# Batching the probability-times-value products of two attention layers over all query blocks of a pair of heads

## The chip, the cores and the metric

The kernel runs on one core of a Trainium2 chip. The metric is device time in microseconds (us) of one execution. Before the change, three runs took 2350.43, 2351.89 and 2341.58 us, median 2350.43. The execution that was profiled took 2338.97 us; its span from the first to the last instruction is 2337.0 us, so 1.97 us lie around the span.

## The reference, cut to what matters

A float32 network on 512 tokens of width 1024: a recurrent layer, an MLP, an attention layer with forget gates ("fox", 16 heads of 64), an MLP, a hybrid layer ("nsa", 8 query heads that share 2 key/value heads, in three branches, beside a short convolution), an MLP. The change touches the probability-times-value products of fox and of two of the three nsa branches. For one block of 128 queries fox computes

```python
logits = einsum('bhqd,bhkd->bhqk', q[:, :, s:e], k[:, :, :e]) * scale
logits = logits + (c[:, :, s:e, None] - c[:, :, None, :e])
p = softmax(where(causal, logits, -inf), axis=-1)
outs.append(einsum('bhqk,bhkd->bhqd', p, v[:, :, :e]))
```

so query block i sees the key blocks 0 to i. In nsa the selected branch picks all 8 blocks of 64 keys, and the window (512) covers the sequence; both are causal attention over the same 512 keys with different keys and values, a linear distance bias and a gate per query and head. The third branch attends to 31 compressed keys.

## The kernel before, in words

Activations lie feature-major, 128 features by 512 tokens in a tile. The large projections multiply fp32 data as three fp32r products (high by high, high by low, low by high): L146, L147, L149 in `proj_fm` with 512 moving columns, L266 to L268 in `proj_tm` with 256. Their weights arrive by DMA (`wr`) and are split into `wh` on ScalarE (L91, L95) and `wl` on VectorE (L92, L96).

Attention goes by pair of heads: 8 pairs in fox (`attend`), 4 in nsa (`nsa_attend`), where each pair runs the branches b = 0 (selected) and b = 1 (window). There are thus 8 + 8 = 16 groups, each of four query blocks i (128 queries) and two heads. One row of work, for one head and one query block of width (i+1) x 128 keys, is: two score products into PSUM bank "s" (L497/L498, L743/L744); VectorE adds the bias and takes the minimum (L331); ScalarE takes the exponential (L339); VectorE the reciprocal (L342); GpSimd scales (L343); then `p_rows` transposes the i+1 blocks by fp32 products with the identity (L363) into bank "t" and copies them to a tile `pt` of 512 columns (6 buffers, L365), by ScalarE for the first head of the pair and by VectorE for the second. In fox GpSimd also builds the bias tile D (L500, L502). D, E and the broadcast gates cb share the 6 buffers of tag "sc".

After both heads of a query block, `pv2` (L373) multiplies: for each key block, for each of the two heads, one fp32 product of the 64 columns of V (stationary) with 128 columns of `pt` (moving). The two heads write to partitions 0 to 63 and 64 to 127 of the PSUM bank O. The trace records each fp32 product twice (two passes), so a query block has 4(i+1) records and a group 40. In nsa the compressed branch first writes O with one product of 512 columns for each head (L737, the tile `pc`, from the tag "pt"). When O is complete, `o_parts` splits it into a high part (ScalarE, L379) and a low part (VectorE, L380), which the output projection reads. O has one buffer.

The rows are interleaved with other work by generators: in fox with the projections of the following heads and, for the last two pairs, with the output projection `out1`; the rest of it, `out2`, comes after the last pair. In nsa each of the 32 yields of attention alternates with one of `nsa_conv`. The fox loop goes through i = 3, 2, 1, 0 with the heads inside; the nsa loop through i = 0 to 3 with b inside, and the transposes that prepare the next pair (`stack`) stand after i = 1 of branch 1. `stack` also issues four DMAs on SP.

The program text is not the order on the engines: the tile framework orders the instructions itself when the program is built, on a simulated timeline (L1666, `schedule_with_timeline_sim=True`), and sets the semaphores. Once built, each engine's order is fixed.

Of the kernel before, what the change touches and what calls it, by code (L numbers as in the profile page):

```python
# [9 lines left out]
F32 = mybir.dt.float32  # L10
# [8 lines left out]
P = 128  # L19
D = 1024  # L20
T = 512
# [10 lines left out]
class Net:  # L32
# [322 lines left out]
                next(fill, None)  # L355
                done += 1

    def p_rows(self, pool, E, n, eng):

        tb = self.bank("t")  # L360
        w = n * P
        for j in range(n):
            self.nc.tensor.transpose(tb[:, j * P:(j + 1) * P], E[:, j * P:(j + 1) * P], self.ident)  # L363
        pt = pool.tile([P, T], F32, tag="pt", bufs=6, name=self.nm("pt"))
        eng(pt[:, :w], tb[:, :w])  # L365
        return pt

    def pv2(self, O, n, V, pts, i, first=True, last=True):


        for b in range(n):
            for j in range(2):
                self.nc.tensor.matmul(O[64 * j:64 * j + 64, i * P:(i + 1) * P], V(j, b), pts[j][:, b * P:(b + 1) * P],  # L373
                                      start=first and b == 0, stop=last and b == n - 1)

    def o_parts(self, O, oh, ol):

# [4 lines left out]
    def fox(self):  # L382
        nc, tc, a = self.nc, self.tc, self.a
        with tc.tile_pool(name="fox", bufs=2, reuse_waits="tile") as fp, \
# [4 lines left out]
            f, u, s2, q = [fp.tile([P, 4 * H], F32, name=f"f{n}") for n in "fusq"]  # L389
# [57 lines left out]
            tb = self.bank("t")  # L447
# [5 lines left out]
            c = self.sc("fc")[:H]  # L453
# [4 lines left out]
            tb = self.bank("t")  # L458
# [17 lines left out]
            def attend(m):  # L476

                cc, j = divmod(m, 2)
                v = st["v", cc]
                ks, qs = st["kq", m]  # L480
                oh = fp.tile([P, T], F32R, tag="oh", bufs=NK, name=self.nm("oh"))
                ol = fp.tile([P, T], F32R, tag="ol", bufs=NK, name=self.nm("ol"))
                O8.append((oh, ol))
                cbs = []
                for hh in range(2):
                    cb = self.sc("cb")
                    nc.sync.dma_start(cb, cd[2 * m + hh:2 * m + hh + 1, :].partition_broadcast(P))
                    cbs.append(cb)
                O = self.bank("o")
                for i in range(3, -1, -1):  # L490
                    wd = (i + 1) * P
                    pts = []
                    for hh in range(2):
                        h = 2 * m + hh
                        S = self.bank("s")
                        qa, qb = qs[hh]
                        nc.tensor.matmul(S[:, :wd], qa[:, i * P:wd], ks[hh][:, :wd], start=True, stop=False)  # L497
                        nc.tensor.matmul(S[:, :wd], qb[:, i * P:wd], ks[hh][:, :wd], start=False, stop=True)  # L498
                        Dt = self.sc("D")
                        nc.gpsimd.tensor_scalar(Dt[:, :wd], cbs[hh][:, :wd], 1.0, nct[:, i * H + h:i * H + h + 1],  # L500
                                                op0=ALU.mult, op1=ALU.add)
                        nc.gpsimd.affine_select(Dt[:, i * P:wd], Dt[:, i * P:wd], pattern=[[-1, P]],  # L502
                                                compare_op=ALU.is_ge, fill=BIG, base=0, channel_multiplier=1)
                        E = self.softmax_row(fp, S, Dt[:, :wd], wd, 1.0)
                        pts.append(self.p_rows(fp, E, i + 1, nc.vector.tensor_copy if hh else nc.scalar.copy))
                        if hh:
                            self.pv2(O, i + 1, lambda c, b: v[:, b, 128 * j + 64 * c:128 * j + 64 * c + 64], pts, i)
                            if i == 0:
                                self.o_parts(O, oh, ol)
                        yield  # L510


# [168 lines left out]
    def nsa_attend(self, fp, e, O4):  # L681

        nc = self.nc
        gt, v = e["gt"], e["v"]
        qs = []

        def stack(m):
            qs.extend(self.q_stack(fp, self.fm_bank(e["q"][m // 2], (m % 2) * P, 256), e["gq"]))
        def compressed(h):

            g = h // 4
            qa, qb = qs[h]
            Dch = fp.tile([P, P], F32, tag="Dch", bufs=2, name=self.nm("Dch"))
            nc.gpsimd.tensor_scalar(Dch, e["Dc"].rearrange("p t c -> p (t c)"), 2.0 ** -(h + 1), 0.0, op0=ALU.mult,
                                    op1=ALU.add)
            S = self.bank("s")
            for i in range(4):
                r = slice(i * P, (i + 1) * P)
                o = S[:, 32 * i:32 * i + 32]
                nc.tensor.matmul(o, qa[:, r], e["kc"][g], start=True, stop=False)  # L700
                nc.tensor.matmul(o, qb[:, r], e["kc"][g], start=False, stop=True)
            E = fp.tile([P, P], F32, tag="Ec", bufs=2, name=self.nm("Ec"))
            E3 = E.rearrange("p (t c) -> p t c", t=4)
            m4 = fp.tile([P, 3, 4], F32, tag="m4", bufs=2, name=self.nm("m4"))
            nc.vector.tensor_tensor(E, S[:, :P], Dch, op=ALU.add)
            nc.vector.tensor_reduce(m4[:, 0], E3, axis=AX.X, op=ALU.min)
            nc.vector.tensor_scalar(m4[:, 0], m4[:, 0], 1e20, None, op0=ALU.min)
            nc.vector.tensor_tensor(E3, E3, m4[:, 0, :, None].to_broadcast([P, 4, 32]), op=ALU.subtract)
            nc.scalar.activation(E, E, AF.Exp, scale=-1.0)
            nc.vector.tensor_reduce(m4[:, 1], E3, axis=AX.X, op=ALU.add)  # L710
            nc.vector.tensor_scalar(m4[:, 1], m4[:, 1], 1e-30, None, op0=ALU.max)
            nc.vector.reciprocal(m4[:, 2], m4[:, 1])
            nc.vector.tensor_tensor(m4[:, 2], m4[:, 2], gt[:, :, h], op=ALU.mult)
            nc.vector.tensor_tensor(E3, E3, m4[:, 2, :, None].to_broadcast([P, 4, 32]), op=ALU.mult)
            tb = self.bank("t")
            for i in range(4):
                nc.tensor.transpose(tb[:32, i * P:(i + 1) * P], E3[:, i], self.ident)
            pc = fp.tile([P, T], F32, tag="pt", bufs=6, name=self.nm("pc"))[:32]
            nc.scalar.copy(pc, tb[:32])
            return pc  # L720

        stack(0)
        for hp in range(4):
            g = hp // 2
            hv = slice(g * 64, g * 64 + 64)
            Dh = []
            for h in (2 * hp, 2 * hp + 1):
                Dh.append(fp.tile([P, T], F32, tag="Dh", bufs=3, name=self.nm("Dh")))
                nc.gpsimd.tensor_scalar(Dh[-1], e["D0"], 2.0 ** -(h + 1), 0.0, op0=ALU.mult, op1=ALU.add)
            O = self.bank("o")  # L730
            for i in range(4):
                wd = (i + 1) * P
                for b in range(2):
                    if i == b == 0:
                        pcs = [compressed(h) for h in (2 * hp, 2 * hp + 1)]
                        for j in range(2):
                            nc.tensor.matmul(O[64 * j:64 * j + 64], e["vc"][:, hv], pcs[j], start=True, stop=False)  # L737
                    pts = []
                    for j in range(2):
                        h = 2 * hp + j  # L740
                        qa, qb = qs[h]
                        S = self.bank("s")
                        nc.tensor.matmul(S[:, :wd], qa[:, i * P:wd], e["ks"][b][g][:, :wd], start=True, stop=False)  # L743
                        nc.tensor.matmul(S[:, :wd], qb[:, i * P:wd], e["ks"][b][g][:, :wd], start=False, stop=True)  # L744
                        E = self.softmax_row(fp, S, Dh[j][:, T - wd:], wd, 1.0,
                                             gate=gt[:, i, 8 * (b + 1) + h:8 * (b + 1) + h + 1])
                        pts.append(self.p_rows(fp, E, i + 1, nc.vector.tensor_copy if j else nc.scalar.copy))
                    self.pv2(O, i + 1, lambda j, n: v[:, n, 128 * b + 64 * g:128 * b + 64 * g + 64], pts, i, first=False,
                             last=b == 1 and i == 3)
                    if i == 1 and b and hp < 3:  # L750
                        stack(hp + 1)
                    if i == 3 and b:
                        self.o_parts(O, *O4[hp])
                    yield
# [916 lines left out]
```

## Time and profile before

| what | value |
| --- | --- |
| three runs, median | 2350.43 us (2341.58 to 2351.89) |
| profiled execution / its span | 2338.97 / 2337.0 us |
| PE busy (matmul) | 2239.0 us, 96% |
| VectorE, ScalarE, GpSimd busy | 1367.7, 945.0, 568.1 us |
| DMA traffic | 237.37 MB, 102 GB/s on average |
| the chain that ended last | PE 82%, DVE 5%, DMA 2% |

PE is TensorE's matmul, PEld its weight load, DVE VectorE, ACT ScalarE, POOL GpSimd, SP SyncE. Matmuls overlap in the array and their ends are modelled, so the time from one start to the next tells more than the duration of a record. A timeline row merges like records that follow each other: the first number is the start, the second the length until the last one's end, and "xN" the count of records. The fox attention lies at about 905 to 1131 us of the span and the nsa attention at 1570 to 1830 us.

### The profile page before, as it was taken

Reading aid. Unit: us, or ns where it says so; the run is one execution under the profiler, and the core shown is the slowest. Engines: PE = TensorE matmul, PEld = TensorE weight load, DVE = VectorE, ACT = ScalarE, POOL = GpSimd, SP = SyncE. Lnnn points to the kernel's source line nnn. Section 1 sums busy time; section 2 is a strip of 40 time slices with the busy share of each in tenths; the row PEclk is TensorE's granted clock in tenths of the full one; section 3 lists DMA queues with packets and bytes.
Section 4 is the critical chain, followed back from the end, with each engine's and each line's share of the span. In section 5 each row is a group of like instructions: output and inputs, shape, how many; then the busy total and the mean of one; then the engine's idle time right before and its main releaser. Section 6 shows DMA issues by size and latency. Waiting matters only on the chain.

```text
span 2337.0 us, 33070 instructions
## 1 busy us (share of the span) xinstructions
PE 2239.0 (96%) x12545; PEld 1856.5 (79%) x12545; DVE 1367.7 (59%) x2718; ACT 945.0 (40%) x1928; POOL 568.1 (24%) x655
## 2 busy tenths in 40 slices
PE   4988877999999999999999999999999999999999
PEld 4767666778888889987788888897777888888887
DVE  8997778664444467765744444755554445444444
ACT  5575455343322345654523324344334324332331
POOL 6554235221021012444220120303331102012010
PEclk9998888999999999999999999999999999999999
DMA  3158634213232233332323223232223433223322
GB/s 124 39 163 252 176 94 131 65 41 106 90 105 93 92 102 108 98 83 71 104 93 105 91 95 104 75 116 73 84 84 104 135 108 109 90 90 100 99 91 81
DMA packets 104015, 237.37 MB, mean 102 GB/s; under 512 B 9664, under 2 KB 42176, under 8 KB 103856
## 3 DMA queue, kind: packets, MB, share of 16 engines
q1 hardware_dynamic: 73712, 214.28, 28.8%
q10 hardware_dynamic: 30144, 20.98, 3.0%
q8 instruction: 99, 1.62, 0.3%
q14 instruction: 60, 0.49, 0.1%
HBM read 210.02 MB, written 18.91 MB: 98 GB/s over the span
## 4 chain that ended last, share of the span: by engine, by line
PE 82%; DVE 5%; DMA 2%; ACT 1%; issue 1%; POOL 0%; ACTq 0%; SPq 0%; DVEq 0%; POOLq 0%
PE psacc L146 20%; PE psacc L149 20%; PE psacc L147 20%; PE pso L373 2%; PE psacc L268 2%; PE psacc L266 2%; PE psacc L267 2%; PE pst L363 2%; DVE wl L92 1%; PE pso L1447 1%; PE pso L1449 1%; PE pso L1448 1%; DMA xh<-in_x_dram 0%; PE pss L497 0%; PE pss L744 0%
## 5 line engine op out<-in xcount | busy, mean ns | idle before, releaser
L91 ACT CAST wh<-wr 128x512 fp32r<-128x512 f32 (+1 forms) x593 | 324.2, 617 | 470.7 <-PE psacc L149 341.2
L92 DVE TENSOR_TENSOR wl<-wr,wh 128x512 fp32r<-128x512 f32 (+1 forms) x581 | 422.1, 778 | 38.7 <-ACT wh L91 35.8
L146 PE MATMUL psacc<-xg,wh 128*128 128x512 f32 x1104 | 432.6, 392 | 0.0
L147 PE MATMUL psacc<-xg,wl 128*128 128x512 f32 x1104 | 432.1, 391 | 0.0
L149 PE MATMUL psacc<-xgl,wh 128*128 128x512 f32 x1104 | 431.2, 392 | 0.4 <-DVE xgl L176 0.4
L146 PE MATMUL psacc<-hid,wh 128*128 128x512 f32 x768 | 299.7, 393 | 0.0
L149 PE MATMUL psacc<-hidl,wh 128*128 128x512 f32 x768 | 299.1, 392 | 0.0
L147 PE MATMUL psacc<-hid,wl 128*128 128x512 f32 x768 | 298.5, 391 | 0.0
L254 POOL TENSOR_TENSOR xall<-xall,yt 128x512 f32<-128x512 f32 x72 | 107.7, 1495 | 666.3 <-DVE yt L253 666.3
L149 PEld LDWEIGHTS psacc<-xgl,wh 128*128 128x128 f32 x1104 | 207.2, 188 | 44.7 <-DVE xgl L176 1.5
L147 PEld LDWEIGHTS psacc<-xg,wl 128*128 128x128 f32 x1104 | 207.4, 188 | 42.4 <-issue 0.9
L146 PEld LDWEIGHTS psacc<-xg,wh 128*128 128x128 f32 x1104 | 207.4, 188 | 42.2 <-issue 0.5
L253 DVE TENSOR_TENSOR yt<-psacc,rb 128x512 f32<-128x512 f32 x96 | 66.4, 692 | 273.3 <-PE psacc L149 273.3
L241 DVE TENSOR_TENSOR ht<-ht,psacc 128x512 f32<-128x512 f32 x96 | 66.1, 688 | 224.2 <-ACT ht L240 224.0
L240 ACT ACTIVATE ht<-psacc 128x512 f32<-128x512 f32 x96 | 57.6, 600 | 280.2 <-PE psacc L149 280.1
L149 PEld LDWEIGHTS psacc<-hidl,wh 128*128 128x128 f32 x768 | 144.2, 188 | 32.7
L147 PEld LDWEIGHTS psacc<-hid,wl 128*128 128x128 f32 x768 | 144.2, 188 | 32.0
L146 PEld LDWEIGHTS psacc<-hid,wh 128*128 128x128 f32 x768 | 144.2, 188 | 31.5
L266 PE MATMUL psacc<-wh,xg 128*128 128x256 f32 (+2 forms) x504 | 144.3, 287 | 1.7 <-ACT gt L647 1.5
L268 PE MATMUL psacc<-wh,xgl 128*128 128x256 f32 (+2 forms) x504 | 144.0, 286 | 0.6 <-DVE gq L593 0.6
L267 PE MATMUL psacc<-wl,xg 128*128 128x256 f32 (+2 forms) x504 | 144.3, 287 | 0.0
L200 POOL TENSOR_TENSOR ssacc<-ssacc,sq 128x512 f32<-128x512 f32 x35 | 53.0, 1516 | 228.2 <-ACT sq L199 227.2
(492 smaller groups left out, 4067.0 us busy)
## 6 DMA issues: line engine op xcount, KB each, us to landing
wr<-in_mlp_in_dram SPq DMA_DIRECT2D x96, 512.0 KB, 4.2
wr<-in_mlp_out_dram SPq DMA_DIRECT2D x96, 512.0 KB, 4.3
dQ<-q ACTq DMA_DIRECT2D x8, 1024.0 KB, 5.9
wr<-in_w_q_dram SPq DMA_DIRECT2D x12, 512.0 KB, 3.8
wr<-in_rw_k_dram SPq DMA_DIRECT2D x8, 512.0 KB, 3.8
wr<-in_rw_r_dram SPq DMA_DIRECT2D x8, 512.0 KB, 3.3
wr<-in_rw_v_dram SPq DMA_DIRECT2D x8, 512.0 KB, 4.8
wor<-in_rw_o_dram SPq DMA_DIRECT2D x8, 512.0 KB, 3.6
```

The source lines that it names most:

```text
L91: nc.scalar.copy(h, r)
L92: (eng or nc.vector).tensor_tensor(wl[:rows, b:f], r, h.bitcast(F32), op=ALU.subtract)
L146: nc.tensor.matmul(ps_, wi[0], xh, start=i == 0, stop=False)
L147: nc.tensor.matmul(ps_, wi[1], xh, start=False, stop=False)
L149: nc.tensor.matmul(ps_, wi[0], xl, start=False, stop=i == n - 1)
L240: nc.scalar.activation(t, ps, AF.Relu)
L241: nc.vector.tensor_tensor(t, t, ps, op=ALU.mult)
L253: nc.vector.tensor_tensor(t, ps, r2, op=ALU.mult)
L254: (nc.vector if q == 3 else nc.gpsimd).tensor_tensor(self.xs[m], self.xs[m], t, op=ALU.add)
L266: nc.tensor.matmul(o, xh[:, b], wh, start=kt == 0, stop=False)
L267: nc.tensor.matmul(o, xh[:, b], wl, start=False, stop=False)
L268: nc.tensor.matmul(o, xl[:, b], wh, start=False, stop=kt == NK - 1)
```

## The change

The transposed probabilities of a whole group (four query blocks, two heads) go into one tile PT of 20 blocks of 128 columns (2 buffers, 10 KB per partition each, where six `pt` tiles of 2 KB were). The blocks of one head and one key block lie side by side in the order of the queries, so that `pv2` can run once for each group: for each key block b and each head (the second head first) one product with 128 x (4-b) moving columns, into the columns of O from b x 128 on. That makes 8 products for a group, of 512, 384, 256 and 128 columns, where there were 20 of 128. The copies out of bank "t" write with a step of 5 or 6 blocks. In nsa the loops over i and b change places, the call of `stack` is now after six of a pair's eight units (before: four), and `pc` takes a buffer of "sc". The number of scores, softmax instructions, transposes and copies stays the same.

```diff
--- before.py
+++ after.py
@@ -355,23 +355,29 @@
                 next(fill, None)
                 done += 1
 
-    def p_rows(self, pool, E, n, eng):
-
-        tb = self.bank("t")
-        w = n * P
-        for j in range(n):
-            self.nc.tensor.transpose(tb[:, j * P:(j + 1) * P], E[:, j * P:(j + 1) * P], self.ident)
-        pt = pool.tile([P, T], F32, tag="pt", bufs=6, name=self.nm("pt"))
-        eng(pt[:, :w], tb[:, :w])
-        return pt
-
-    def pv2(self, O, n, V, pts, i, first=True, last=True):
-
-
-        for b in range(n):
-            for j in range(2):
-                self.nc.tensor.matmul(O[64 * j:64 * j + 64, i * P:(i + 1) * P], V(j, b), pts[j][:, b * P:(b + 1) * P],
-                                      start=first and b == 0, stop=last and b == n - 1)
+    def p_tile(self, pool):
+        return pool.tile([P, 20, P], F32, tag="PT", bufs=2, name=self.nm("PT"))
+
+    def p_rows(self, E, PT, j, i, eng):
+
+
+
+        tb, n = self.bank("t"), i + 1
+        for k in range(n):
+            c = i - k if j else k
+            self.nc.tensor.transpose(tb[:, k * P:(k + 1) * P], E[:, c * P:(c + 1) * P], self.ident)
+        o, d = (15 - 5 * i, 6) if j else (i + 1, 5)
+        eng(PT[:, o:o + d * i + 1:d], tb[:, :n * P].rearrange("p (k q) -> p k q", q=P))
+
+    def pv2(self, O, V, PT, first=True, last=True):
+
+
+        for b in range(4):
+            for j in (1, 0):
+                o = 5 * (3 - b) if j else 6 * b + 1
+                self.nc.tensor.matmul(O[64 * j:64 * j + 64, b * P:], V(j, b),
+                                      PT[:, o:o + 4 - b].rearrange("p n q -> p (n q)"),
+                                      start=first and b == 0, stop=last and b == 3)
 
     def o_parts(self, O, oh, ol):
 
@@ -486,10 +492,9 @@
                     cb = self.sc("cb")
                     nc.sync.dma_start(cb, cd[2 * m + hh:2 * m + hh + 1, :].partition_broadcast(P))
                     cbs.append(cb)
-                O = self.bank("o")
+                O, PT = self.bank("o"), self.p_tile(fp)
                 for i in range(3, -1, -1):
                     wd = (i + 1) * P
-                    pts = []
                     for hh in range(2):
                         h = 2 * m + hh
                         S = self.bank("s")
@@ -502,11 +507,10 @@
                         nc.gpsimd.affine_select(Dt[:, i * P:wd], Dt[:, i * P:wd], pattern=[[-1, P]],
                                                 compare_op=ALU.is_ge, fill=BIG, base=0, channel_multiplier=1)
                         E = self.softmax_row(fp, S, Dt[:, :wd], wd, 1.0)
-                        pts.append(self.p_rows(fp, E, i + 1, nc.vector.tensor_copy if hh else nc.scalar.copy))
-                        if hh:
-                            self.pv2(O, i + 1, lambda c, b: v[:, b, 128 * j + 64 * c:128 * j + 64 * c + 64], pts, i)
-                            if i == 0:
-                                self.o_parts(O, oh, ol)
+                        self.p_rows(E, PT, hh, i, nc.vector.tensor_copy if hh else nc.scalar.copy)
+                        if hh and i == 0:
+                            self.pv2(O, lambda c, b: v[:, b, 128 * j + 64 * c:128 * j + 64 * c + 64], PT)
+                            self.o_parts(O, oh, ol)
                         yield
 
 
@@ -715,7 +719,7 @@
             tb = self.bank("t")
             for i in range(4):
                 nc.tensor.transpose(tb[:32, i * P:(i + 1) * P], E3[:, i], self.ident)
-            pc = fp.tile([P, T], F32, tag="pt", bufs=6, name=self.nm("pc"))[:32]
+            pc = self.sc("pc")[:32]
             nc.scalar.copy(pc, tb[:32])
             return pc
 
@@ -728,14 +732,14 @@
                 Dh.append(fp.tile([P, T], F32, tag="Dh", bufs=3, name=self.nm("Dh")))
                 nc.gpsimd.tensor_scalar(Dh[-1], e["D0"], 2.0 ** -(h + 1), 0.0, op0=ALU.mult, op1=ALU.add)
             O = self.bank("o")
-            for i in range(4):
-                wd = (i + 1) * P
-                for b in range(2):
+            for b in range(2):
+                PT = self.p_tile(fp)
+                for i in range(4):
+                    wd = (i + 1) * P
                     if i == b == 0:
                         pcs = [compressed(h) for h in (2 * hp, 2 * hp + 1)]
                         for j in range(2):
                             nc.tensor.matmul(O[64 * j:64 * j + 64], e["vc"][:, hv], pcs[j], start=True, stop=False)
-                    pts = []
                     for j in range(2):
                         h = 2 * hp + j
                         qa, qb = qs[h]
@@ -744,11 +748,12 @@
                         nc.tensor.matmul(S[:, :wd], qb[:, i * P:wd], e["ks"][b][g][:, :wd], start=False, stop=True)
                         E = self.softmax_row(fp, S, Dh[j][:, T - wd:], wd, 1.0,
                                              gate=gt[:, i, 8 * (b + 1) + h:8 * (b + 1) + h + 1])
-                        pts.append(self.p_rows(fp, E, i + 1, nc.vector.tensor_copy if j else nc.scalar.copy))
-                    self.pv2(O, i + 1, lambda j, n: v[:, n, 128 * b + 64 * g:128 * b + 64 * g + 64], pts, i, first=False,
-                             last=b == 1 and i == 3)
+                        self.p_rows(E, PT, j, i, nc.vector.tensor_copy if j else nc.scalar.copy)
                     if i == 1 and b and hp < 3:
                         stack(hp + 1)
+                    if i == 3:
+                        self.pv2(O, lambda j, n: v[:, n, 128 * b + 64 * g:128 * b + 64 * g + 64], PT, first=False,
+                                 last=b == 1)
                     if i == 3 and b:
                         self.o_parts(O, *O4[hp])
                     yield
```

## Rows read from the trace of the kernel before

**Rows 1.** The page: busy time by engine, then PE and PEclk in 40 slices.

```profile
span 2337.0 us, 33070 instructions
...
PE 2239.0 (96%) x12545; PEld 1856.5 (79%) x12545; DVE 1367.7 (59%) x2718; ACT 945.0 (40%) x1928; POOL 568.1 (24%) x655
...
PE   4988877999999999999999999999999999999999
...
PEclk9998888999999999999999999999999999999999
```

**Rows 2.** Fox, nsa attention: length; busy PE, PEld, DVE, ACT, POOL; PEclk, DMA share, GB/s.

```profile
905.00:1131.00 226.00, 223.13 (x1638) 193.17 (x1636) 152.60 (x462) 129.47 (x326) 91.72 (x187) 1.00 0.31 90
...
1570.00:1830.00 260.00, 260.00 (x1469) 203.62 (x1469) 143.85 (x418) 105.42 (x264) 70.86 (x97) 1.00 0.28 89
```

**Rows 3.** Chain that ended last, by line: 905 to 1131 us, then 1570 to 1830 us.

```profile
by line: PE pso L373 12.9%; PE psacc L267 12.9%; PE psacc L266 12.7%; PE psacc L268 12.7%; PE pst L363 8.5%; PE psacc L146 5.0%; PE psacc L149 5.0%; PE psacc L147 5.0%; PE pss L497 4.7%; PE pss L498 4.7%; DMA qa<-qa 2.8%; PE pst L296 2.8%; 
...
by line: PE psacc L149 22.6%; PE psacc L147 22.6%; PE psacc L146 22.3%; PE pso L373 10.4%; PE pst L363 8.2%; PE pss L744 4.1%; PE pss L743 3.9%; PE pso L737 1.9%; PE pst L717 1.3%; PE pss L701 1.2%; PE pss L700 1.0%; PE pst L296 0.5%
```

**Rows 4.** Line 373, the whole span: records of the products in fox and in nsa.

```profile
L373 PE MATMUL pso<-pt,v x320: 272/273/324, 916.9 to 1123.8; 128*64 128x128 f32 x160
...
L373 PE MATMUL pso<-pt,nv x320: 272/273/324, 1585.8 to 1826.6; 128*64 128x128 f32 x160
```

**Rows 5.** Timeline of PE around three runs of the product: start, length, what.

```profile
916.61 0.28 PE L268 MATMUL psacc<-wh,xgl 128*128 128x256 f32 x1
916.73 0.28 PE L266 MATMUL psacc<-wh,xg 128*128 128x256 f32 x1
916.94 0.43 PE L373 MATMUL pso<-pt,v 128*64 128x128 f32 x2
917.30 0.33 PE L497 MATMUL pss<-ks,qa 128*128 128x128 f32 x1
...
920.15 1.09 PE L373 MATMUL pso<-pt,v 128*64 128x128 f32 x14
921.17 0.55 PE L363 MATMUL pst<-ident,E 128*128 128x128 f32 x3
...
1612.91 0.87 PE L373 MATMUL pso<-pt,nv 128*64 128x128 f32 x10
1613.71 0.55 PE L363 MATMUL pst<-ident,E 128*128 128x128 f32 x3
```

**Rows 6.** Timeline of PE: the 512-column products, heads together, then apart.

```profile
1584.58 1.07 PE L737 MATMUL pso<-pc,vc 32*64 32x512 f32 x4
1585.59 0.33 PE L363 MATMUL pst<-ident,E 128*128 128x128 f32 x1
...
1639.86 1.07 PE L737 MATMUL pso<-pc,vc 32*64 32x512 f32 x2
1640.86 0.33 PE L363 MATMUL pst<-ident,E 128*128 128x128 f32 x1
...
1641.35 1.07 PE L737 MATMUL pso<-pc,vc 32*64 32x512 f32 x2
1642.35 0.43 PE L373 MATMUL pso<-pt,nv 128*64 128x128 f32 x2
```

**Rows 7.** Waits of POOL and of PE in 905 to 1131 us: total, times, longest.

```profile
POOL D L500 <- PE pst L363: 37.7, 12, 8.6
...
PE pso L373 <- DVE pt L365: 0.4, 1, 0.4
```

**Rows 8.** Timeline at the end of fox: DVE, then PE.

```profile
1120.87 2.50 DVE L92 TENSOR_TENSOR wl<-wr,wh 128x512 fp32r<-128x512 f32 x4 [1.39 <-ACT wh L91]
1123.29 0.28 DVE L365 COPY pt<-pst 128x128 f32<-128x128 f32 x1
...
1123.62 0.43 PE L373 MATMUL pso<-pt,v 128*64 128x128 f32 x2 [0.44 <-DVE pt L365]
1124.73 0.50 PE L146 MATMUL psacc<-oh,wh 128*128 128x512 f32 x1 [0.68 <-ACT oh L379]
```

## The prediction

> **What bounds the kernel now.** I began with the page: PE is busy 96% of the span, beside its weight load no engine is above 59%, and the granted clock is nine tenths or more almost everywhere [rows 1]. The change touches two stages only, so the busy time by stretch came next: in the fox attention PE is busy 223.13 of 226 us, in the nsa attention 260.00 of 260, at full clock, that is at 2.4 GHz; VectorE, the second, has 152.60 and 143.85 us there [rows 2]. In both stages PE has work at every moment, so a microsecond of PE time taken out should be a microsecond of the kernel, as long as the order of the rest holds. The chain of waits says the same and gives the share of the line that changes: L373 holds 12.9% of the fox stretch (29.2 us) and 10.4% of the nsa stretch (27.0 us), together 56.2 us [rows 3]. The reader should see that this is far from negligible for 640 records [rows 4], and that the question is what part of it is arithmetic.
>
> **What a product costs.** For that I read starts on the timeline of PE, not durations. The run of 14 records lasts from 920.15 to the next start at 921.17, 1.02 us; the run of 10 lasts 0.80 us (1612.91 to 1613.71); the run of 2 lasts 0.36 us (916.94 to 917.30) [rows 5]. Four records more cost 0.22 us: two products, four passes of 128 columns. One product alone is two passes, so 0.22 us is the time of one product; the second one ran beside it, in the other half of the array's columns. I call this 0.22 us a slot (0.217 to three digits, which fits the runs of 2, 10 and 14 alike): one key block by 128 queries, of both heads. A run costs its slots plus about 0.15 us: 1.02 - 4 x 0.217, and 0.36 - 0.217 gives the same. Entering a run costs more: the fp32r product ahead of it starts at 916.73 and the run at 916.94, 0.21 us, where the one before took 0.12 us (916.61 to 916.73), so 0.09 us [rows 5].
>
> The run of 2 followed by 14 also shows the order that is kept in the bank O: the first head's block 0 goes alone, because its copy is ready first; the rest waits for the second head and then runs as second head's block 0 beside first head's block 1, and so on, the last one alone again. A query block of n key blocks thus takes n+1 slots: 2+3+4+5 = 14 slots for a group instead of 10.
>
> **Part 1: fewer, longer products.** Removed: 56.2 us by the chain, in 100 runs (counted over the two stretches: 48 of 2 records, 11 of 6, 9 of 14, 9 of 10 and some others). Summing the runs by their lengths gives 58.6 us; I take the lower. Entering them: 100 x 0.09 = 9.0 us, which the lines ahead of them carry. Added: 16 groups with 4+3+2+1 = 10 slots, 10 x 0.217 + 0.15 = 2.32 us, if each group is one run and the heads are side by side; 37.1 us, and 16 x 0.09 = 1.4 us to enter. Here the second head comes first; it is the one copied last, so all 16 records are ready together, and the keeping of order in O that split the runs before now keeps them in one.
> No row shows a product of 128 rows with 512 columns, so I bound it. The nearest is L737, also fp32 with 64 stationary columns, 512 moving: four records, both heads, take 1.01 us from start to next start (1584.58 to 1585.59) [rows 6], which is 4 x 0.217 + 0.14. That is the favourable bound and the nearest row, and I take it. The other bound is the same line in the next pair: two records of one head alone take 1.00 us, twice (1639.86, 1641.35) [rows 6], because score products stood between them. Then the group has 20 slots: 20 x 0.217 + 0.15 = 4.49 us, 71.8 us in all.
> The Trainium skill has a rule against the favourable bound: "TensorE: Matmul & The Clock Gate", Part 3, section on packing small matmuls, says that a weight load overlaps matmuls in flight only where its row group differs. Both heads use all 128 rows, so by this rule they would take turns, and the sum would be the unfavourable one; the row of four records in 1.01 us disagrees, with two heads of one row group.
> Net of this part: 56.2 + 9.0 - 37.1 - 1.4 = 26.7 us less.
>
> **Part 2: the products move to the end of the group.** The queue behind them on PE is fixed: while PE stands before the first product of a group, transposes, scores and projections behind it stand too. Before, PE's waits on VectorE's copies for L373 in the fox stage were 0.4 us in all [rows 7], and in nsa PE has no idle time [rows 2]; there are 16 such meeting points now instead of 64. Inside the stages I cost this at nothing, the cover being the projections (in fox) and the convolution (in nsa); without that cover a group waits up to 2.4 us (VectorE's four weight splits from 1120.87 to the copy at 1123.29) [rows 8].
> At the end of fox there is no cover. The last copy starts at 1123.29, the last run of 2 at 1123.62, then ScalarE's split of O, then `out2` at 1124.73 [rows 8]. After the change the whole group of 2.32 us stands there instead of 0.36: 2.0 us later, and the bounds are nothing (if the last softmax comes that much earlier) and 4 us (the same plus the earlier rows' products, which now fill no wait). I take 2.0. At the end of nsa the next reader of O comes after two projections of eight input tiles each, and I cost it at nothing.
>
> **Part 3: copies, buffers, loop order.** Copies stay 128 and keep their columns; the step in the output goes in whole blocks of 128. VectorE and ScalarE are not full, so I take nothing; between -0.1 and +0.1 us a copy would hide there too. PT has room for one group ahead, which is more than the 6 `pt`. `pc` now takes two of the 6 "sc" buffers for the short time until O is free; in nsa nothing else but E uses them then. `stack` after six units instead of four leaves two units, some 16 us (260 us / 32 x 2), for its four copies by DMA and the SP queue ahead of them; in nsa PE waits for none of this now. Nothing, with 0 to 2 us as bounds for all three.
>
> **Sum.** -26.7 + 2.0 = -24.7, about 25 us. Against the profiled execution 2338.97 - 25 = 2314. That execution was 11.5 us under the median and even under the lowest of the three runs, so for the median I subtract from 2350.43: **2325 us**. A change under 0.5%, 12 us here, cannot be told from none.
>
> **Rivals.**
> Torn runs: the order is written again at build time, and other instructions may come between the two heads, as in L737's second pair. Each group that loses its 512-column pair loses 0.87 us plus 0.25 us for one run more; half of the groups 9 us, all 18 us, so a gain of 16 to 7 us: 2334 to 2343, say 2338. For it: one such case in the few rows; against it: the order kept in O. Chance 0.16.
> Fox becomes bound by its softmax chain: GpSimd waited 37.7 us for transposes to free "sc" buffers [rows 7], and a run of 2.32 us delays transposes. Then fox gives back its half, 13 us: 2338. Against it: VectorE is busy 152.60 of 226 us. Chance 0.08.
> Heads take turns at these lengths, one waiting until the other's passes are through: 71.8 + 1.4 against 65.2 us, 8.0 more, with the tail 10 more at most, 2356 to 2360. Against it: both heads in 1.01 us [rows 6]. Chance 0.05. The skill's rule in part 1 would bring this about.
> The other side, PE stands at the group's first product for the last copy: 2.4 us a group [rows 8] is 38 us, less 25: 13 slower, 2363. It decides from 25/16 = 1.6 us a group on, and is slower by over 0.5% from 2.3 us. For it: VectorE's weight splits do stand ahead of copies at the end of fox; against it: 0.4 us in all that stage [rows 7]. Chance 0.09, of which 0.06 beyond 0.5%.
>
> **How the numbers follow.** Forecast 0.62. Lower end: gain of 29 us (58.6 instead of 56.2 us removed, tail nothing) from the profiled 2339: 2310. Upper end: the torn and the fox rival, and the slower of the runs, 2346; what lies above is 0.14. Faster by over 0.5% (below 2338.7): 0.62, 0.09 of torn, 0.04 of fox: 0.75. Slower: 0.06. Rest 0.19.
>
> **What would show it.** Right: L373 with 256 records, in 16 runs of 16, each 2.3 us to the next start, heads starting within 0.01 us of each other; the fox stretch 12 us shorter, the nsa stretch 13. Wrong: records of one head alone, runs of fewer than 16, PE idle before L373 by copies (`PT`) of over 1 us a group, or a fox stretch no shorter while GpSimd waits more.

## The result, and the profile after

The changed kernel takes 2316.38 us (median of 4 runs, 2310.41 to 2320.74) against 2346.01 us (4 runs): a ratio of 0.9871, interval [0.9834, 0.9908]. Timed again beside the experiments, it came to 0.9872 [0.9853, 0.9891] of the kernel before. The profiled execution took 2310.41 us, 28.6 us under the one of before.

The page of the changed kernel, the lines that answer to [rows 1]:

```profile
span 2308.7 us, 32324 instructions
...
PE 2206.2 (96%) x12161; PEld 1832.3 (79%) x12161; DVE 1371.0 (59%) x2718; ACT 942.0 (41%) x1928; POOL 568.6 (25%) x655
```

PE has 384 records less and is as full as before; VectorE, ScalarE and GpSimd are busy within 3.3 us of before. Line 378 is the product now (line 373 before), 256 records in four lengths where [rows 4] had 640 of one:

```profile
L378 PE MATMUL pso<-PT,v x128: 272/432/643, 936.2 to 1107.2; 128*64 128x512 f32 x32, 128*64 128x384 f32 x32, 128*64 128x256 f32 x32, 128*64 128x128 f32 x32
...
L378 PE MATMUL pso<-PT,nv x128: 272/432/644, 1595.8 to 1799.6; 128*64 128x512 f32 x32, 128*64 128x384 f32 x32, 128*64 128x256 f32 x32, 128*64 128x128 f32 x32
```

The timeline of PE shows one run for a group, here one of fox and one of nsa (compare [rows 5]):

```profile
935.89 0.34 PE L503 MATMUL pss<-ks,qb 128*128 128x384 f32 x1
936.16 2.38 PE L378 MATMUL pso<-PT,v 128*64 128x512 f32 x16
938.46 0.66 PE L368 MATMUL pst<-ident,E 128*128 128x128 f32 x4
...
1595.46 0.40 PE L147 MATMUL psacc<-xg,wl 128*128 128x512 f32 x1
1595.79 2.37 PE L378 MATMUL pso<-PT,nv 128*64 128x512 f32 x16
1598.09 0.65 PE L368 MATMUL pst<-ident,E 128*128 128x128 f32 x4
```

936.16 to 938.46 and 1595.79 to 1598.09 are 2.30 us each. All 16 runs have 16 records, and 15 of them take 2.30 to 2.31 us to the next start; the last of fox has a wait behind it. In the chain of waits L378 holds 9.0% of a fox stretch of 206 us and 7.5% of an nsa stretch of 245 us, 18.5 and 18.4 us, where [rows 3] had 29.2 and 27.0:

```profile
by line: PE psacc L266 13.7%; PE psacc L267 13.4%; PE psacc L268 13.3%; PE pso L378 9.0%; PE pst L368 7.7%; PE psacc L146 5.4%; PE psacc L147 5.2%; PE psacc L149 4.8%; PE pss L503 4.6%; PE pss L502 4.5%; DMA qa<-qa 3.1%; PE pst L296 2.1%; D
...
by line: PE psacc L146 23.5%; PE psacc L147 23.4%; PE psacc L149 23.4%; PE pso L378 7.5%; PE pst L368 7.5%; PE pss L747 4.3%; PE pss L748 4.2%; PE pso L742 2.4%; PE pst L721 1.5%; PE pss L705 1.1%; PE pss L704 0.9%; PE pst L296 0.5%
```

To see where the time went I cut the span at the MLPs, whose products (`hid`) open and close each of them. First the kernel before, then the changed one: start of the first and of the last of the records of a line, by MLP.

```profile
L149 PE MATMUL psacc<-hidl,wh x256: 389/389/476, 552.8 to 857.2; 128*128 128x512 f32 x128
L146 PE MATMUL psacc<-hid,wh x256: 388/394/475, 1177.6 to 1483.9; 128*128 128x512 f32 x128
L149 PE MATMUL psacc<-hidl,wh x256: 388/392/477, 1178.1 to 1484.4; 128*128 128x512 f32 x128
L146 PE MATMUL psacc<-hid,wh x256: 392/396/398, 2022.4 to 2331.5; 128*128 128x512 f32 x128
```

```profile
L149 PE MATMUL psacc<-hidl,wh x256: 389/389/476, 554.4 to 858.8; 128*128 128x512 f32 x128
L146 PE MATMUL psacc<-hid,wh x256: 387/394/475, 1160.9 to 1467.3; 128*128 128x512 f32 x128
L149 PE MATMUL psacc<-hidl,wh x256: 388/392/477, 1161.5 to 1467.8; 128*128 128x512 f32 x128
L146 PE MATMUL psacc<-hid,wh x256: 392/396/398, 1993.8 to 2302.9; 128*128 128x512 f32 x128
```

Fox lies between the end of the first MLP and the start of the second: 857.2 to 1177.6, 320.4 us before, 302.1 after. Nsa lies between the second and the third: 538.0 and 526.0 us. That is 18.3 and 12.0 us, 30.3 in all; the MLPs are as long as before, and the recurrent stage ahead took 1.6 us more. The same cuts serve for every experiment, because they leave out the recurrent stage, whose code no kernel here touches and whose length differs from run to run (below).

### The profile page after: what moved, and what is told of

Its sections match the earlier page's. It is cut to its first block, busy times and chain, and to the rows that moved or that the text cites. A ratio compares the mean times of both kernels' runs of the same rounds, so it can differ in the third digit from the quotient of the medians.

```text
span 2308.7 us, 32324 instructions
## 1 busy us (share of the span) xinstructions
PE 2206.2 (96%) x12161; PEld 1832.3 (79%) x12161; DVE 1371.0 (59%) x2718; ACT 942.0 (41%) x1928; POOL 568.6 (25%) x655
## 3 DMA queue, kind: packets, MB, share of 16 engines
q8 instruction: 96, 1.57, 0.3%
## 4 chain that ended last, share of the span: by engine, by line
PE 82%; DVE 6%; DMA 2%; ACT 1%; issue 1%; POOL 0%; ACTq 0%; SPq 0%; DVEq 0%; POOLq 0%
PE psacc L146 20%; PE psacc L149 20%; PE psacc L147 20%; PE psacc L266 3%; PE psacc L268 2%; PE psacc L267 2%; PE pso L378 2%; PE pst L368 1%; DVE wl L92 1%; DVE xgl L176 1%; PE pso L1452 1%; PE pso L1454 1%; PE pso L1453 1%; PE pss L747 0%; PE pss L748 0%
## 5 line engine op out<-in xcount | busy, mean ns | idle before, releaser
L266 PE MATMUL psacc<-wh,xg 128*128 128x256 f32 (+2 forms) x504 | 144.6, 287 | 2.7 <-ACT gt L651 1.6
```

Of the source, the lines that this page charges most:

```text
L266: nc.tensor.matmul(o, xh[:, b], wh, start=kt == 0, stop=False)
```

## The experiments

The theory (A in the expectations): what is paid is slots (0.217 us for one key block of both heads, or of one head if it is alone) and runs (0.15 us each, and 0.09 us to enter one). The rival B: long products are cheaper than short ones. The rival C: the order of the heads is of no account, because the array finds the other half's work by itself. Lengths of the two stages in the profiles, in us, cut as above. Behind them stands PE's time in both stages, split in three: the products of the line that changes and all other instructions of PE, each from its start to the next start without idle time, and PE's waits (idle stretches of over 0.06 us). What it costs to enter a run is in the second of these columns.

```
kernel                              fox    nsa    sum    runs   products  others  waits
before                             320.4  538.0  858.4   100     58.8     794.3    5.3
changed                            302.1  526.0  828.1    16     36.9     783.1    8.2
changed, once more                 302.4  527.7  830.1    16     36.9     784.7    8.4
second head first, before's shape  310.7  530.3  841.0    62     44.4     788.3    8.2
short products, first version      307.7  540.8  848.5    52     46.5     791.3   10.8
short products, one run a group    305.9  526.7  832.6    16     37.5     784.6   10.5
first head first                   310.4  529.9  840.3    27     48.7     784.3    7.2
heads one after the other, long    313.7  537.5  851.2    16     61.8     781.9    7.5
heads one after the other, short   318.1  541.2  859.3    16     66.2     784.4    8.8
small edits                        304.8  525.1  829.9    16     36.9     783.5    9.4
```

In six of these profiles the granted clock fell for a short time at the start of nsa, in two of the six also once in fox (last section). The changed kernel's nsa was 1.7 us longer with such a fall than without, so differences of that size between two rows say nothing.

### One line in the kernel before: the second head first

```diff
         for b in range(n):
-            for j in range(2):
+            for j in (1, 0):
                 self.nc.tensor.matmul(O[64 * j:64 * j + 64, i * P:(i + 1) * P], V(j, b), pts[j][:, b * P:(b + 1) * P],
```

> The kernel before with one edit: pv2 takes the second head first; products stay 20 of 128 columns for a group, row by row. Theory A (slots and runs: 0.217 us for a key block of both heads, 0.15 us a run and 0.09 us to enter it): no head is alone any more, 160 slots instead of some 208, and about 62 runs instead of 100, so L373 takes 160 x 0.217 + 62 x 0.24 = 49.6 us of PE instead of 71: the span some 21 us under before, three quarters of the gain, 8 to 10 us over the changed kernel. Rival B (fewer, longer products pay): nothing is longer here, so within 5 us of before.

Timed: 0.9936 [0.992, 0.9952]. The stages are 17.4 us shorter than before, 57% of the change's 30.3. The runs are as expected, 62, each whole and paired; a run of 8 (two key blocks) and one of 16 (four):

```profile
937.99 0.66 PE L373 MATMUL pso<-pt,v 128*64 128x128 f32 x8
938.58 0.33 PE L363 MATMUL pst<-ident,E 128*128 128x128 f32 x1
...
947.82 1.09 PE L373 MATMUL pso<-pt,v 128*64 128x128 f32 x16
948.84 0.38 PE L268 MATMUL psacc<-wh,xgl 128*128 128x256 f32 x1
```

0.59 and 1.02 us to the next start. All runs together take 44.4 us where A's 160 slots and 62 x 0.15 us make 44.0; in the kernel before they take 58.8. The other lines of PE got 6.0 us shorter, and PE waited 2.9 us longer, mostly on the DMA of qa and qb (2.5 against 1.0 us) and on copies ahead of products (1.5 against 0.6). No product is longer than before, so B, which expected next to nothing, falls; A holds, but its 21 us were too much by 3.6, chiefly these waits, which it had not charged. The span fell by only 12.5 us, since the recurrent stage was 4.7 us longer in this profile.

### The changed kernel with short products

```diff
-        for b in range(4):
-            for j in (1, 0):
-                o = 5 * (3 - b) if j else 6 * b + 1
-                self.nc.tensor.matmul(O[64 * j:64 * j + 64, b * P:], V(j, b),
-                                      PT[:, o:o + 4 - b].rearrange("p n q -> p (n q)"),
-                                      start=first and b == 0, stop=last and b == 3)
+        for i in range(4):
+            for b in range(i + 1):
+                for j in (1, 0):
+                    o = (5 * (3 - b) if j else 6 * b + 1) + i - b
+                    self.nc.tensor.matmul(O[64 * j:64 * j + 64, i * P:(i + 1) * P], V(j, b), PT[:, o],
+                                          start=first and b == 0, stop=last and b == i and (first or i == 3))
```

> The changed kernel, with the group's products cut into 20 of 128 columns again, still one run at the group's end, second head first. Theory A: the run of 40 records lasts as long as the run of 16, 10 x 0.217 + 0.15 = 2.3 us, the span is that of the changed kernel within 2 us. Rival B (each product has a cost of its own, so 12 products fewer for a group are the gain): the runs last longer, up to where half of the gain is gone: 15 us over the changed kernel.

Timed: 0.995 [0.9933, 0.9967], with stages 20.4 us over the changed kernel's, so at first sight B's case. The runs say otherwise. In fox all eight groups are one run of 40 records, and in seven of them it takes hardly longer than 16 long ones, 938.33 to 940.66, 2.33 us. In nsa the text begins with query block 0, which is ready first there, and the order written at build time tore the groups into 44 runs:

```profile
938.33 2.40 PE L379 MATMUL pso<-PT,v 128*64 128x128 f32 x40
940.66 1.09 PE L368 MATMUL pst<-ident,E 128*128 128x128 f32 x8
...
1599.61 0.65 PE L379 MATMUL pso<-PT,nv 128*64 128x128 f32 x6
1600.19 1.09 PE L368 MATMUL pst<-ident,E 128*128 128x128 f32 x8
1601.22 0.65 PE L379 MATMUL pso<-PT,nv 128*64 128x128 f32 x6
```

So this kernel didn't keep the runs equal and could not decide between A and B. The eighth group, at half the clock, is told of in the last section. The second version goes through the query blocks of nsa from the last to the first, so that the products are ready together in both stages (of its edit the line that differs; the flag that ends the sum in O moves with it):

```diff
+        for i in (range(4) if first else range(3, -1, -1)):
```

> As the run with 20 products of 128 columns, but in nsa the query blocks go in the order in which the last-made one comes first, so that the group's products are ready together and stay one run there too. Theory A (slots and runs, not the count of products): every group 2.3 us, nsa within 2 us of the changed kernel's 526 us (the first version had 541 us, with 44 runs), the ratio to before within 0.003 of the changed kernel's. Rival B (fewer, longer products pay): nsa over 532 us although the runs are whole.

Timed: 0.9881 [0.9862, 0.9899], against 0.9872 [0.9853, 0.9891] for the changed kernel timed beside it: no difference that can be told. All 16 groups are one run of 40, 942.26 to 944.59, 2.33 us:

```profile
942.26 2.40 PE L379 MATMUL pso<-PT,v 128*64 128x128 f32 x40
944.59 1.09 PE L368 MATMUL pst<-ident,E 128*128 128x128 f32 x8
```

Nsa took 526.7 us, as A expected. Fox took 305.9, 3.5 us over its neighbour. The runs explain 0.3 of that and longer waits of PE 2.1 (on the DMA of qa 2.7 against 1.6 us, on `raw` 1.7 against 1.1); the rest lies in PE's other lines. Why the waits are longer is not shown. In the runs themselves 12 products fewer for a group are worth 0.02 us a group, 0.6 us in both stages: the length of the products buys next to nothing; the run does.

### The changed kernel with the first head first

```diff
-            for j in (1, 0):
+            for j in (0, 1):
```

> The changed kernel with the first head first in pv2. Theory A (products into one bank keep their order, and the first head's copy is done a softmax earlier): the first head's 512-column product goes ahead alone in most groups, which costs 4 slots and a run more, 0.87 + 0.24 = 1.1 us in 11 to 16 of 16 groups: 12 to 18 us over the changed kernel, at 0.997 to 0.994 of before. Rival (the order of the heads is of no account, the array pairs them anyway): same as the changed kernel within 2 us.

Timed: 0.9921 [0.9901, 0.9941]. The stages are 12.2 us over the changed kernel's first profile and 10.2 over its second, which like this one has the fall of the clock in nsa. In 11 of the 16 groups the first head's 512 columns went ahead alone:

```profile
937.73 1.07 PE L378 MATMUL pso<-PT,v 128*64 128x512 f32 x2
938.74 0.38 PE L268 MATMUL psacc<-wh,xgl 128*128 128x256 f32 x1
...
941.06 2.37 PE L378 MATMUL pso<-PT,v 128*64 128x512 f32 x14
943.36 1.09 PE L368 MATMUL pst<-ident,E 128*128 128x128 f32 x8
```

1.01 us alone, and the other 14 records still need 2.30: 11 x 1.1 = 12.1 us by A. The runs of all groups together are 11.8 us longer than in the changed kernel (48.7 against 36.9). This is the kernel before's fault in another shape, and the rival (no account) falls.

### The heads one after the other

Long products, then short ones (the loop over the heads outermost, the rest as in the kernels above):

```diff
-        for b in range(4):
-            for j in (1, 0):
+        for j in (1, 0):
+            for b in range(4):
```

> The changed kernel with all four products of the second head ahead of all four of the first. Theory A (two heads run side by side only where their products are next to each other): 20 slots for a group, 4.5 us a run instead of 2.3, the span 35 us over the changed kernel and 3 to 8 us over before. Rival C (the array looks further ahead and finds the other half's work): the runs stay below 3 us and the span within 10 us of the changed kernel.

Timed: 0.9977 [0.9966, 0.9989]. Neither expectation: a run takes 3.86 us (934.73 to 938.59), between 2.3 and 4.5, and the stages are 23.1 us over the changed kernel; the runs are 16 x 1.55 = 24.8 us longer.

```profile
934.73 3.93 PE L378 MATMUL pso<-PT,v 128*64 128x512 f32 x16
938.59 0.66 PE L368 MATMUL pst<-ident,E 128*128 128x128 f32 x4
```

In the program as built, all 16 groups have the text's order on PE: four products of the second head, then four of the first. Yet in the single records the first head's first pass of 512 columns starts (936.292) 5 ns behind a pass of the second head (936.287) that has three passes of its head still to come. So the array does find work of the other half that stands behind, but not far. The short version measures how far:

> Products of 128 columns, one run for each group, all ten of the second head ahead of all ten of the first. In the run with long products in this order, the first head's first pass started beside the third-last... pass of the second head, when three records of it were still to come. Reading 1 (the array looks ahead by a fixed count of records): the overlap is again three or four passes, now of 128 columns: a run of some 36 passes, 36 x 0.1085 + 0.15 = 4.1 us. Reading 2 (it looks ahead as far as the time of the passes in that run, about 0.9 us): eight passes overlap, 32 x 0.1085 + 0.15 = 3.6 us. Reading 3 (no limit that matters): 2.3 us.

```profile
934.01 4.20 PE L379 MATMUL pso<-PT,v 128*64 128x128 f32 x40
938.14 1.09 PE L368 MATMUL pst<-ident,E 128*128 128x128 f32 x8
```

934.01 to 938.14 is 4.13 us in 15 of the 16 groups: reading 1, a few records and not a time. Again the first head starts when three of the second's records are still to come, and again the built order is the text's. This kernel was timed once; its stages are 31.2 us over the changed kernel, with a fall of the clock more.

### Two small edits on top

```diff
-                        for j in range(2):
+                        for j in (1, 0):
                             nc.tensor.matmul(O[64 * j:64 * j + 64], e["vc"][:, hv], pcs[j], start=True, stop=False)
...
-                        self.p_rows(E, PT, hh, i, nc.vector.tensor_copy if hh else nc.scalar.copy)
+                        self.p_rows(E, PT, hh, i, nc.vector.tensor_copy if hh and (m < 7 or i) else nc.scalar.copy)
```

> The changed kernel with two small edits that follow from theory A: the compressed products of nsa also take the second head first (in the changed kernel two of the four pairs ran apart, 1.00 us lost in each and a run more), and in fox's last row of the last pair both copies go to ScalarE, since VectorE's copy stood behind weight splits while PE waited 0.88 us. Theory A: nsa 2 to 2.5 us shorter, the wait before the last group of fox under 0.5 us; in all 2 to 3 us under the changed kernel, too little for the timed runs. Rival (schedule noise decides at this size): no change in the stage lengths that can be put down to either.

and its neighbour, the changed kernel again:

> The changed kernel once more, as the neighbour of the other runs of this call: 0.985 to 0.990 of before; from MLP to MLP fox 302 us and nsa 526 us, while the recurrent stage ahead of them, the same program in all of these kernels, may differ by some us from run to run.

Timed: 0.9873 [0.9853, 0.9894] and 0.9872: equal, as the size of the edits foretold. In the stages the first edit did what it should. The neighbour has two pairs of compressed products apart, as in [rows 6], the edited kernel none; first the neighbour, then the edited kernel:

```profile
1625.52 1.07 PE L742 MATMUL pso<-pc,vc 32*64 32x512 f32 x2
1626.51 0.50 PE L147 MATMUL psacc<-xg,wl 128*128 128x512 f32 x1
...
1630.86 1.07 PE L742 MATMUL pso<-pc,vc 32*64 32x512 f32 x2
1631.86 0.39 PE L747 MATMUL pss<-ks,qa 128*128 128x256 f32 x1
```

```profile
1636.79 1.07 PE L742 MATMUL pso<-pc,vc 32*64 32x512 f32 x4
1637.79 0.39 PE L748 MATMUL pss<-ks,qb 128*128 128x256 f32 x1
```

Nsa is 525.1 against 527.7 us. The second edit missed: on ScalarE the last copy stands behind casts of the next MLP's weights just as it stood behind VectorE's splits, and PE waits longer, 1.90 us against 1.15 in the neighbour:

```profile
1108.62 0.26 ACT L370 COPY PT<-pst 128x128 f32<-128x128 f32 x1
1108.78 1.14 ACT L91 CAST wh<-wr 128x512 fp32r<-128x512 f32 x2
1109.83 0.26 ACT L370 COPY PT<-pst 128x128 f32<-128x128 f32 x1
...
1110.14 2.37 PE L378 MATMUL pso<-PT,v 128*64 128x512 f32 x16 [1.90 <-ACT PT L370]
```

## Why the prediction was right, point by point

**What bounds the stages.** Right in the main: PE time taken out came out of the kernel. By the table the products fell by 21.9 us, PE's other lines, which carry the time to enter a run, by 11.2, and PE's waits grew by 2.9: 30.2 us, and the stages gave 30.3. So not quite one for one: a tenth of what PE saved went into longer waits.

**Part 1, the added runs.** Right to a hundredth: 2.32 us forecast, 2.31 measured, 15 times (the last run of fox has the wait for the split behind it). Taking the favourable bound from L737 was right for 128 rows as well. The Trainium skill's rule in "TensorE: Matmul & The Clock Gate", Part 3 (a weight load overlaps matmuls in flight only where the row group differs), does not describe this case: PE is busy for 96% of the changed kernel's span and its weight loads for 79%, nearly all with all 128 rows, so most of the loads did overlap matmuls. That the heads would take turns was my reading of that rule; two heads of one row group ran side by side in every kernel here that put their products next to each other. The kernel with the heads one after the other took 3.86 us a run, and even there they overlapped in part.

**Part 1, the removed runs.** The mis-sized term. I took 56.2 us, the share of L373 in the chain, and 9.0 - 1.4 = 7.6 us for entering fewer runs. The runs from start to next start, without the waits in them, make 58.8 us, and PE's other lines fell by 11.2 us. The sum by run lengths that stood beside it, 58.6, was nearer. Of the 11.2, some 8.5 are an estimate of the entering itself (the record ahead of each run, its time to the run's start without waits, less the median of such records elsewhere: 0.1 us a run). The rest was not forecast, and where all of it lies is not shown; the transposes alone got 4.5 us shorter (L363, now L368).

**Part 1, which half pays.** The prediction named two causes, lone heads and runs. Both are shown: the order of the heads alone, in the kernel before, brings 17.4 us (lone heads, and 38 runs fewer); the step from there to the changed kernel, 62 runs merged into 16, brings the other 12.9. The loop order in nsa, `PT` and the place of `stack` came with that step and were not tried apart. The length of the products, by which the change is described, brings next to nothing: 40 short records take 2.33 us, 16 long ones 2.31.

**Part 2, the end of fox.** I added 2.0 us because 2.32 us of products stand there instead of 0.36. That counted the products twice, since part 1 already held them. What may be added is only the growth of the wait. Before, PE waited there 0.20 us, and 0.44 and 0.68 in [rows 8], 1.32 in all; now

```profile
1105.05 2.37 PE L378 MATMUL pso<-PT,v 128*64 128x512 f32 x16 [0.88 <-DVE PT L370]
1108.11 0.50 PE L146 MATMUL psacc<-oh,wh 128*128 128x512 f32 x1 [0.69 <-ACT oh L385]
```

1.57 us: 0.25 more. Fox moved ahead as a whole, its last softmax with it. The other 2.6 us by which PE's waits grew lie elsewhere, in fox on `raw` (1.1 against 0.2) and on the DMA of qa and qb (1.6 against 1.0) above all, and were put at nothing; that the 2.0 came near the 2.9 of all waits is luck. So the sum was 5.6 us short of the 30.3 through part 1: 26.7 us forecast, 33.1 measured (21.9 and 11.2), from which the 2.9 of waits go off.

**Split and part 3.** I expected 12 us of fox and 13 of nsa; it was 18.3 and 12.0. Part of that was arithmetic: by its own terms, with 56 runs in fox and 44 in nsa, the prediction comes to about 13.0 and 11.7. Beyond that, fox had more lone heads (31 runs of a single product against 17). The copies at nothing was right: their medians are 414 ns on ScalarE and 483 on VectorE, before 416 and 479. In nsa the compressed products cost 1.0 us more, since two pairs ran apart where before it was one, and PE's waits grew by 0.6 us; both were put at nothing.

**The rivals.** Torn runs did not come in the changed kernel, but the first short version and the kernel with the first head first show that they are real, 10 to 15 us; in these kernels the run stayed whole where the order of the heads and of the blocks put first the product that is ready last. Fox bound by its softmax: GpSimd's wait for transposes did grow, from 37.7 to 47.2 us, but fox got shorter all the same. PE waiting for the last copy: only at the end of fox, 0.9 to 1.9 us over the kernels that keep this shape, never the 1.6 us a group from which it would have decided.

**The number.** 2325 us was forecast, 25 us under the median of before; it is 2316.38, inside the range and 29.6 us under the median of before, which came to 2346.01 with a fourth run. Of the 8.6 us between forecast and result 4.4 are thus the base and 4.2 the gain. A range of 36 us would have held a gain half as large too; what bears the mechanism out are the 16 whole runs of 2.31 us and the experiments.

## What to carry to other kernels

Read PE's timeline by starts and group it into runs of one array shape: here each run of 64-column products cost some 0.24 us beside its passes (an estimate from [rows 5]), and a head without a partner cost its whole length. Two half-width products shared the array in full only where they stood next to each other in PE's order, so write first the one that is ready last; here nothing came between then. When work is moved to the end of a stage, charge the wait that grows there, not the work, if the work is already in the sum.

## What the runs showed that I had not expected

**PE starts matmuls out of the order of the program, a few records deep.** The trace shows starts, and the built program the order: with all of one head's products ahead of the other's, the second in line started beside a pass that had three more of its own head behind it, with passes of 512 to 128 columns and with passes of 128 alike (3.86 and 4.13 us where taking turns would be 4.5 by the slots).

**A wait of PE can be followed by a lower clock, and need not be.** In the first short version PE stood idle ahead of fox's last group. Stretches of that kernel: length, busy PE, PEld, DVE, ACT and POOL, granted clock, DMA share, GB/s:

```profile
1105.00:1108.00 3.00, 3.00 (x16) 2.46 (x15) 1.36 (x3) 0.41 (x1) 0.71 (x2) 1.00 0.91 313
1108.00:1111.00 3.00, 1.26 (x7) 0.71 (x5) 1.35 (x3) 2.00 (x5) 0.00 (x0) 1.00 0.64 242
1111.00:1113.00 2.00, 1.80 (x23) 1.80 (x25) 1.35 (x3) 0.34 (x1) 0.00 (x0) 0.72 0.46 143
1113.00:1116.00 3.00, 2.32 (x21) 1.92 (x20) 0.21 (x1) 0.58 (x1) 0.00 (x0) 0.62 0.82 268
```

PE was busy 1.26 of 3.00 us, then the granted clock fell to 0.72 and 0.62 in these stretches, that is to 1.2 GHz for part of each, and the run of 40 took 3.93 us where it takes 2.40 elsewhere:

```profile
1111.20 3.93 PE L379 MATMUL pso<-PT,v 128*64 128x128 f32 x40 [1.94 <-DVE PT L370]
```

The wait alone does not decide it: in the kernel with the small edits PE waited 1.90 us at the same place and the clock stayed at 1.00, while in the middle of its fox a wait of 1.9 us on the DMA of qa was followed by 0.57 from 1010 to 1014 us. At the start of nsa PE waits 1.4 to 1.6 us (L266) in all ten profiles; the clock fell there in six and not in the other four. The changed kernel has one of either kind, first with the fall, then without, and its nsa took 527.7 and 526.0 us:

```profile
1505.00:1509.00 4.00, 3.44 (x15) 3.44 (x16) 0.73 (x1) 1.05 (x4) 0.00 (x0) 0.57 0.41 131
...
1505.00:1509.00 4.00, 2.42 (x19) 2.28 (x19) 1.98 (x3) 2.29 (x6) 0.00 (x0) 1.00 0.39 124
```

**The recurrent stage is where the runs differ.** The first product of the first MLP starts between 551.6 and 559.5 us over these ten profiles, with the same code ahead of it, while each MLP keeps its length to 0.1 us. A difference of 8 us that has nothing to do with an edit hides a quarter to a half of gains of 17 to 30 us in a single span; the cuts at the MLPs show it.
